# Float32 weights in four column groups of the array for the samples' and adaLN products, and a rebuilt first stretch, in a two-layer hybrid decoder step

## The chip, the cores and the metric

The kernel runs on 1 core of one Trainium2 chip. The metric is the device time in microseconds (us). A NeuronCore has five engines with a queue each: TensorE (PE for its products, PEld for its weight loads), VectorE (DVE), ScalarE (ACT), GpSimd (POOL) and SyncE (SP). SP issues all DMAs here. Every engine works through its own queue in order; semaphores tie them together.

## The reference

One inference step of a two-layer decoder on a prompt of 4096 tokens and on 8 samples of one token each, all in float32, width 1024. What matters here:

```python
shift, scale, gate = split(silu(c) @ ada_w[layer] + ada_b[layer], 3)   # adaLN, 9 rows of c: 8 samples, 1 prompt
h = rmsnorm(x, g_pre) * (1 + scale) + shift
# layer 0: three groups of 4 heads, (window, dilation) = (128,1), (512,4), (2048,16)
q, k, v, z = split(h @ w_in_a, 4);  out = (mixture of the three dilated attentions * silu(z)) @ w_o_a
# layer 1: 16 query heads, 2 shared key/value heads, window 128, sinks
kv = (rmsnorm(x, g_kv) * (1 + kv_scale) + kv_shift) @ w_kv
q, z = split(h @ w_in_b, 2);  out = (attention(q, kv, sinks) * silu(z)) @ w_o_b
x = x + gate * rmsnorm(out, g_post)          # after each layer
```

The prompt and the samples go through the same weights; the samples' keys and values also enter caches that are returned.

## The kernel before

The prompt is cut into 32 tiles of 128 rows. Seven passes follow each other: A0, A1, A2 (layer 0, one head group each: dilation 16, 4, 1), C (the output projection of layer 0), B0, B1 (layer 1, eight query heads each) and D (its output projection). Each pass runs over the 32 tiles. A tile's main work on TensorE is 48 products of 128x128 by 128x512 (36 in C): float16 high and low parts of the activations (`xT`) and weights (`wt`), three products per chunk of 128 input columns, eight chunks, two halves. That makes 32 x (6 x 48 + 36) = 10368 products, written on line 641 (line 634 in the changed file).

The order of the work on every engine is written out by hand. The dictionaries `PA0`, `PA`, `PL`, `PC`, `PB0`, `PB1`, `PD` give each step of a tile a tick; a tile has 48 ticks, in which its 48 products are laid out evenly; step `tq=69` of a tile thus stands in the next tile's ticks. Instructions are issued to the queues in order of ticks. Beside the tiles runs one generator per pass, `side`: all that concerns the 8 samples, the adaLN vectors of later layers, and the splitting of the next pass's weights into float16 parts. It is advanced by one `yield` every `PACE[pi]` ticks, from tile 1 to tile 29; what is left of it when tile 29 ends is issued at once, between two tiles.

The products of the side work have 9 rows of activations (8 samples and the prompt's row). `weights_pass` and `ada_units` load a float32 tile `st` of two chunks of 128x512 weights (512 KB, two buffers), `split_raw` makes from each chunk a high part (ACT, L225) and a low part (POOL, L226) of type fp32r in `wr`, and two products per chunk with a stationary operand of 41 columns (the high parts of the 9 rows in columns 0 to 8, their low parts in 32 to 40) add up in PSUM; `sum_rows` (L215, L218) adds the two row groups of the result. There are 212 such chunks: 64 issued in A0, 48 in A1, 44 in A2, 24 in C (8 of them 256 wide), 16 in B0 and 16 in B1. Where a pass's weights are split, `scan` first reads them all once for their norm (L255).

The first stretch has no tiles to run beside: `begin_loads` fetches the adaLN weights for the first layer's scale and shift (16 x 512 KB); `ada_row` splits them (ACT L465, DVE L466) and makes two rows from them; `begin_scale` reads the weights of A0 for their norm and multiplies them by the shift (`ps_b`, 16 float32 products of full width); `begin_split` makes A0's float16 weights (L299, L300). The first product of tile 0 follows.

At the end of a weights pass the prompt's row of the result goes out to DRAM (`bd`, L408) and comes back spread over 128 partitions (`bias_b`, L414), and DVE takes its maximum (L416): these set the next pass's scales.

## Time and profile before

| | us |
|---|---|
| median of 3 runs | 3180.49 (3174.47 to 3181.64) |
| the profiled execution | 3164.79 |
| its span, first to last instruction | 3162.7 |
| PE / DVE / ACT / POOL busy in the span | 2967.8 / 2248.5 / 1997.1 / 1151.8 |
| mean granted TensorE clock | 0.981 of 2.4 GHz |

A row of the trace that groups instructions reads: line, engine, operation, output<-inputs by the program's names, shapes, count, then busy time and the mean duration of one, then the idle time of that engine just before them and what ended it. A busy time is a union of intervals; products overlap in the pipeline, so the pitch from one start to the next, and not the duration of a record, says what one costs.

### The profile page before, as it was taken

The numbers are of one execution on the slowest core, as the hardware profiler recorded it, in microseconds if no ns is written. First come the engines' busy times: TensorE is split into PE (matmuls) and PEld (weight loads), VectorE is DVE, ScalarE is ACT, GpSimd is POOL, SyncE is SP. The second block draws the span as 40 slices with busy tenths as digits, with TensorE's granted clock in tenths as the row PEclk, the third lists the DMA queues.
The fourth block names the chain that finished last, engine by engine and source line by source line (L and its number), as shares of the span: only waits on it lengthen the run. The fifth ranks groups of instructions, "written<-read, shape, count | busy, mean of one in ns | idle before, by whom it ended". The sixth has DMA issues, their size and how long they took to land.

```text
span 3162.7 us, 54624 instructions
## 1 busy us (share of the span) xinstructions
PE 2967.8 (94%) x18520; PEld 1554.1 (49%) x18520; DVE 2248.5 (71%) x5056; ACT 1997.1 (63%) x4861; POOL 1151.8 (36%) x1284
## 2 busy tenths in 40 slices
PE   6889989999999999988999899999979999999998
PEld 2444444555455444443444455666645555554444
DVE  6666667666677788885676588998866788874443
ACT  6667777566765676766654467766656787763332
POOL 0445533344333566543442123433222343332221
PEclk8999999999999999999999899999999999999999
DMA  8788997677866788769999478665547887888975
GB/s 226 200 214 228 244 242 193 153 167 163 188 147 159 179 197 184 191 148 258 279 256 251 86 168 169 150 136 136 133 110 157 188 178 156 159 193 234 221 203 162
DMA packets 1092677, 585.68 MB, mean 185 GB/s; under 512 B 925014, under 2 KB 1003367, under 8 KB 1089692
## 3 DMA queue, kind: packets, MB, share of 16 engines
q1 hardware_dynamic: 1092396, 582.19, 76.4%
q8 instruction: 145, 2.38, 0.3%
q14 instruction: 136, 1.11, 0.1%
HBM read 243.61 MB, written 159.30 MB: 127 GB/s over the span
## 4 chain that ended last, share of the span: by engine, by line
PE 29%; DVE 9%; ACT 7%; DMA 5%; issue 5%; SPq 2%; POOL 2%; POOLq 0%; ACTq 0%; DVEq 0%
PE ps_pj L641 17%; PE ps_sc L641 6%; DMA PT<-PS 3%; PE ps_sc L99 2%; ACT P L583 2%; PE ps_o L99 2%; DVE PS L592 1%; PE ps_kv L99 1%; SPq L1337 1%; DVE P L576 1%; DVE pn_t L883 1%; DVE x_t L884 1%; ACT PS L591 1%; ACT xs L163 1%; ACT QTb L1008 1%
## 5 line engine op out<-in xcount | busy, mean ns | idle before, releaser
L641 PE MATMUL ps_pj<-wt,xT 128*128 128x512 f16 x9024 | 2226.9, 383 | 43.3 <-ACT ps_pj L624 36.3
L641 PEld LDWEIGHTS <-xT 128*128 128x128 f16 x10368 | 967.8, 98 | 1028.5 <-issue 114.8
L592 DVE SCALAR_TENSOR_TENSOR PS<-P,PS 128x512 f16<-128x512 f32 (+1 forms) x448 | 435.0, 985 | 145.2 <-ACT PS L591 142.7
L544 POOL TENSOR_TENSOR rope<-rope,rope 128x512 f32<-128x512 f32 x160 | 232.9, 1456 | 668.5 <-DVE rope L539 647.5
L226 POOL TENSOR_TENSOR wr<-st,wr 128x512 fp32r<-128x512 f32 (+1 forms) x212 | 310.3, 1464 | 145.8 <-ACT wr L225 145.2
L624 ACT ACTIVATE ps_pj<-bias,scl 128x512 f32<-128x512 f32 x320 | 219.7, 686 | 217.3 <-DVE gate L552 111.7
L583 ACT ACTIVATE P<-P,nm_b 128x256 f32<-128x256 f32 (+1 forms) x512 | 252.7, 494 | 107.1 <-DVE nm_b L576 106.8
L591 ACT ACTIVATE PS<-P 128x512 f16<-128x512 f32 (+1 forms) x448 | 261.4, 598 | 64.4 <-DMA PT<-PS 60.7
L641 PE MATMUL ps_sc<-wt,xT 128*128 128x512 f16 x1344 | 298.4, 379 | 2.5 <-DMA xT<-usdp 1.5
L576 DVE CUSTOM_DVE_ANT_0 P<-ps_sc,masks,nsink 128x256 f32<-128x256 f32 (+1 forms) x512 | 248.9, 527 | 11.8 <-PE ps_sc L99 11.8
L99 PEld LDWEIGHTS <-PT 128*128 128x128 f16 x3384 | 192.4, 99 | 129.6 <-DMA PT<-PS 38.7
L539 DVE SCALAR_TENSOR_TENSOR rope<-ps_pj,scl,tab 128x512 f32<-128x512 f32 x320 | 224.7, 743 | 25.0 <-PE ps_pj L641 24.0
L576 DVE CUSTOM_DVE_ANT_0 P<-ps_sc,masks,scl 128x256 f32<-128x256 f32 (+1 forms) x384 | 155.4, 449 | 65.1 <-PE ps_sc L99 64.8
L609 DVE TENSOR_REDUCE uo<-ps_o 128x256 f32<-128x512 f32 x224 | 153.2, 684 | 53.2 <-PE ps_o L99 51.5
L99 PE MATMUL ps_sc<-KTb,QTb 128*128 128x256 f16 (+1 forms) x1024 | 154.1, 274 | 21.8 <-ACT QTb L1008 15.8
L1051 POOL TENSOR_TENSOR uo<-uo,gate 128x512 f32<-128x512 f32 x64 | 88.4, 1381 | 189.2 <-PE ps_tr L996 83.1
L143 POOL TENSOR_SCALAR rm_t<-ss 128x1 f32<-128x1 f32 (+2 forms) x132 | 34.8, 264 | 329.1 <-ACT xs L163 288.0
L99 PE MATMUL ps_o<-KV,PT 128*128 128x128 f16 x2016 | 129.7, 208 | 21.3 <-DMA PT<-PS 21.2
L736 DVE COPY KT<-ps_tr 64x512 f16<-64x512 f16 x192 | 81.0, 422 | 93.6 <-ACT KT L734 91.3
L769 POOL TENSOR_TENSOR U<-uo,gate 128x256 f32<-128x256 f32 x96 | 93.6, 975 | 140.2 <-DVE uo L609 138.2
L99 PEld LDWEIGHTS <-QTb 128*128 128x128 f16 x1024 | 97.0, 99 | 87.7 <-ACT QTb L1008 27.3
L583 ACT ACTIVATE P<-P,U 128x256 f32<-128x256 f32 (+1 forms) x256 | 118.1, 462 | 34.2 <-DVE U L576 34.1
(257 smaller groups left out, 4055.1 us busy)
## 6 DMA issues: line engine op xcount, KB each, us to landing
out_a_s_dram<-in_cache_a_kv_g_dram SPq DMA_DIRECT2D x144, 256.0 KB
x_t<-in_x_prompt_dram SPq DMA_DIRECT2D x64, 512.0 KB
st<-in_w_in_a_dram SPq DMA_DIRECT2D x96, 256.0 KB
xsd<-xs SPq DMA_DIRECT2D x32, 512.0 KB
st<-in_ada_w_dram SPq DMA_DIRECT2D x32, 512.0 KB
x1d<-x_t SPq DMA_DIRECT2D x32, 512.0 KB
x1s<-xs SPq DMA_DIRECT2D x32, 512.0 KB
st<-in_w_in_b_dram SPq DMA_DIRECT2D x32, 512.0 KB
```

The costliest lines, as they stand in the source:

```text
L99: nc.tensor.matmul(out, lhsT, rhs, start=start, stop=stop)
L226: nc.gpsimd.tensor_tensor(t[:, 1, :n], raw, t[:, 0, :n], op=ALU.subtract)
L539: nc.vector.scalar_tensor_tensor(t[:n, :w].rearrange("p (h e) -> p h e", e=64), s3, scale, tab[:n, o:o + 64].unsqueeze(1).to_broadcast([n, ...
L544: nc.gpsimd.tensor_tensor(a4, a4, b4[:, :, ::-1, :], op=ALU.add)
L576: nc.vector.tensor_tensor_reduce(out=self.P[:, j, :n], in0=self.sc[:, j, :n], in1=self.mask[:, :n], scale=self.nss, scalar=self.init[j], o ...
L583: nc.scalar.activation(self.P[:, j, :n], self.P[:, j, :n], AF.Exp, bias=self.nm[j], scale=-1.0, accum_out=self.l[j])
L591: nc.scalar.activation(S[:, 0], P, AF.Copy, scale=PSC)
L592: nc.vector.scalar_tensor_tensor(S[:, 1], P, PSC, S[:, 0], op0=ALU.mult, op1=ALU.subtract)
L609: nc.vector.tensor_reduce(out=out.rearrange("p (h e) -> p h e", e=64), in_=ops.rearrange("p h (t e) -> p h e t", t=2), axis=AX.X, op=ALU.add)
L624: nc.scalar.activation(t[f"ps{hf}"], bias[pi, hf], AF.Copy, scale=scl[pi][:, IDS:IDS + 1])
L641: nc.tensor.matmul(t[f"ps{hf}"], t[hT][:, p, c, :], ws()[hf][c][q], start=c == 0 and k == 0 and not biased, stop=c == n - 1 and k == 2, sk ...
L769: nc.gpsimd.tensor_tensor(t["U"][:, :256], t["uo"][:, :256], t["sz"][:, :256], op=ALU.mult)
```

## The change

The side work's products take the float32 weights as they are. The stationary operand is 32 columns wide (9 rows and zeros), and four consecutive chunks go to four groups of 32 columns of the array, each into 32 partitions of the same PSUM tile:

```python
def quarter(ps, hS, c, w, nch):
    q = QR * (c % 4)
    nc.tensor.matmul(ps[q:q + QR, :w.shape[-1]], hS[:, c, :], w, start=c < 4, stop=c + 4 >= nch,
                     tile_position=(0, q))

def sum_quarters(ps, rows, width):
    t = s_half()
    nc.scalar.copy(t[:, :width], ps[:, :width])
    yield
    yield
    o = s_half()
    nc.vector.tensor_tensor(t[:64, :width], t[:64, :width], t[64:128, :width], op=ALU.add)
    nc.vector.tensor_tensor(o[:rows, :width], t[:rows, :width], t[QR:QR + rows, :width], op=ALU.add)
    return o
```

```diff
-    stp = ctx.enter_context(tc.tile_pool(name="st", bufs=2))
+    stp = ctx.enter_context(tc.tile_pool(name="st", bufs=4))
-    wrp = ctx.enter_context(tc.tile_pool(name="wr", bufs=2))
...
-PACE = [3, 4, 4, 6, 6, 6, 13]
+PACE = [4, 5, 4, 8, 6, 6, 13]
...
 weights_pass:
-        staged = [jobs[0][-1](), jobs[1][-1]()]
+        staged = [j[-1]() for j in jobs[:4]]
...
-                for k, p in enumerate(parts):
-                    mm(ps[:SROWS, :n], hS[h][:, c + i, :], p, c + i == 0 and k == 0, last and i == 1024 // n - 1 and k == 1)
+            if len(raw) == 4 or last:
+                for k, w in raw:
+                    quarter(ps, hS[h], k, w, max(j[1] + 1024 // n for j in jobs if j[0] == h))
...
 ada_units:
-            for k in range(8):
-                piece(staged, loads, 8 * u + k, got.append)
+            for k in range(0, 8, 4):
+                yield from wait()
+                for c in range(k, k + 4):
+                    quarter(ps, csr, c, staged[4 * u + c // 2][:, c % 2, :], 8)
...
 first stretch:
-        return [(PA0["load"] - 1, begin_loads), (PA0["load"] + 1, begin_rows), (t + 1, begin_scale), (t + 2, begin_rest)] + [
-            (t + 4 + 3 * j, lambda j=j: begin_split(j)) for j in range(16)] + [
-            (t + 12, lambda: [None for _ in first["qkv"]])]
+        return [(PA0["load"] - 1, begin_c), (PA0["load"] + 1, begin_loads), (t + 1, begin_rows), (t + 2, begin_more),
+                (t + 3, begin_scale), (-1, begin_bias), (16, begin_rest)] + [
+            (t + 4 + 3 * j, lambda j=j: begin_split(j)) for j in range(16)]
+    def first_bias(t, hf):
+        t[f"ps{hf}"] = pj_ps.tile([128, 512], F32, name="ps_pj", tag="pj")
+        nc.tensor.matmul(t[f"ps{hf}"], first["spread"], first["t"][hf], start=True, stop=False, skip_group_check=True)
```

In the first stretch `ada_row` takes unsplit weights too (its ACT and DVE splits are gone), the shift times A0's weights is made by quarters (`ps_q`) and spread over the partitions by a product with `spread`, and that product also writes tile 0's bias into PSUM where ACT did it before; 5 of the 16 squares for the norm move from ACT to DVE. The step tables get new ticks in all passes, by up to 10 ticks in `PA0` and one to eight elsewhere; `PACE` is 4, 5, 4, 8, 6, 6 ticks for A0 to B1.

TensorE in the first stretch, before the first main product; `ps_asc`, `ps_apj` are the two adaLN rows, `wa_hl` the split weights, `ps_b` the shift times A0's weights. Before:

```order
L99 MATMUL ps_asc_455<-wa_hl,csr 41x512 x2
L99 MATMUL ps_asc_456<-wa_hl,csr 41x512 x2
...
L99 MATMUL ps_col<-pick,ada_row_370 128x2 x8
L99 MATMUL ps_z<-wa_1_387,ones 128x512 x2
L99 MATMUL ps_b<-st,S_b 128x512 x16
L99 MATMUL ps_scl<-w_acc,ones 128x16
L641 LDWEIGHTS xT
```

And of the change (`wa` are the weights as loaded; `ps_q` stands in the place of `ps_b`):

```order
L210 MATMUL ps_atr_510<-wa_0_427,csr 32x512
L210 MATMUL ps_atr_510<-wa_0_429,csr 32x512
...
L97 MATMUL ps_col<-pick,ada_row_368 128x2 x8
L210 MATMUL ps_q<-st,S_c 32x512 x16
L97 MATMUL ps_scl<-w_acc,ones 128x16
L1506 MATMUL ps_pj<-s_half,spread_s 128x512 x2
L97 MATMUL ps_b<-s_half,spread 128x512 x2
L634 LDWEIGHTS xT
```

The pairs of split products have become single ones, each on another quarter than its neighbour, and two products for the bias stand before the first main product.

SP's queue in the same stretch; `wa` are the adaLN weights, `st` the weights of A0, `xT<-xs` the first transposed activations. Before:

```order
L431 DMA wa_0_403<-in_ada_w_dram 128x1024
L665 DMA x_t<-in_x_prompt_dram 128x1024
L667 DMA tab<-in_rope_dram 128x128
L325 DMA st<-in_w_in_a_dram 128x2x256 x16
L471 DMA adr_G_341<-ada_row_367 41x1024
L471 DMA adr_S_340<-ada_row_370 41x1024
L665 DMA x_t<-in_x_prompt_dram 128x1024
L667 DMA tab<-in_rope_dram 128x128
L179 DMA_TRANSPOSE xT<-xs 128x16x128
```

And of the change:

```order
L424 DMA wa_0_433<-in_ada_w_dram 128x1024
L658 DMA x_t<-in_x_prompt_dram 128x1024
L660 DMA tab<-in_rope_dram 128x128
L174 DMA_TRANSPOSE xT<-xs 128x16x128
L674 DMA xsd_176<-xs 128x2048
L314 DMA st<-in_w_in_a_dram 128x2x256 x16
L464 DMA adr_G_339<-ada_row_365 9x1024 x4
L464 DMA adr_S_338<-ada_row_368 9x1024 x4
```

The first transposing DMA has moved from behind the loads of A0's weights to ahead of them.

DVE at the end of the samples' work in A0, in the change, between tiles 29 and 30; `wt` are float16 weights of A1, `bias_b` the row that came back from DRAM, `V` and `gate` free the second PSUM half of tile 29. These rows stand there:

```order
L289 SCALAR_TENSOR_TENSOR wt<-st,gw,wt 128x512 [waits DMAHW5_49,Activation_49]
L289 SCALAR_TENSOR_TENSOR wt<-st,gw,wt 128x512 [waits Activation_49]
L219 TENSOR_TENSOR s_half<-s_half 64x512 [waits Activation_49]
L220 TENSOR_TENSOR s_half<-s_half 9x512 [waits DVE_49]
L408 TENSOR_REDUCE b_m<-bias_b 128x1 [waits DMAHW4_49]
...
L600 TENSOR_REDUCE uo<-ps_o 128x256 [waits PE_49]
...
L704 SCALAR_TENSOR_TENSOR V<-ps_pj,scl_602,V 128x4x64 [waits Activation_49]
```

Before, the same sum and the same maximum stood a whole tile apart:

```order
L218 TENSOR_TENSOR s_half<-ps_s,s_half 9x512 [waits Activation_49]
L736 COPY KT_957<-ps_tr 64x4x128 [waits Activation_49]
...
L694 TENSOR_TENSOR QK<-rope_5700,QK 128x8x64 [waits Activation_49]
L609 TENSOR_REDUCE uo<-ps_o 128x256 [waits PE_49]
L416 TENSOR_REDUCE b_m<-bias_b 128x1 [waits DMAHW7_49]
```

In A0 the side work of the change is not done when tile 29 ends, and its rest, 6 splits, 8 quarter products and the trip through DRAM, is issued there in one piece.

## Rows read from the trace of the kernel before

**Rows 1.** Busy time of each engine in the seven passes and ahead of them (the stretches begin with a pass's first main product): stretch, its length, PE, PEld, DVE, ACT, POOL busy with counts, granted clock, DMA share, GB/s.

```profile
0.00:68.00 68.00, 43.38 (x142) 18.96 (x143) 40.31 (x88) 46.91 (x89) 3.16 (x12) 0.88 0.86 239
68.00:543.00 475.00, 434.43 (x2553) 213.57 (x2553) 322.95 (x679) 336.51 (x788) 215.28 (x204) 0.97 0.87 220
543.00:971.00 428.00, 421.94 (x2645) 217.23 (x2644) 287.93 (x641) 270.42 (x663) 156.15 (x126) 1.00 0.70 162
971.00:1433.00 462.00, 434.81 (x2689) 222.33 (x2688) 378.44 (x945) 323.72 (x778) 249.12 (x307) 0.99 0.75 177
1433.00:1717.00 284.00, 268.17 (x1253) 120.03 (x1251) 179.09 (x314) 160.55 (x345) 107.99 (x204) 0.98 0.98 267
1717.00:2292.00 575.00, 548.66 (x4145) 337.92 (x4144) 476.04 (x1144) 368.73 (x988) 183.69 (x151) 0.99 0.64 144
2292.00:2814.00 522.00, 479.08 (x3479) 269.59 (x3477) 409.23 (x990) 370.73 (x968) 160.38 (x129) 0.97 0.75 158
2814.00:3163.00 349.00, 337.29 (x1624) 154.50 (x1622) 154.53 (x259) 119.52 (x248) 76.03 (x156) 0.99 0.79 208
```

**Rows 2.** TensorE's instructions by line, tiles and shape: count, then busy us and mean ns of one, then idle before them.

```profile
L641 PE MATMUL ps_pj<-wt,xT 128*128 128x512 f16 x9024 | 2226.9, 383 | 43.3 <-ACT ps_pj L624 36.3 <-DMA xT<-usdp 4.2 <-DVE pn_t L883 2.8
...
L99 PE MATMUL ps_s<-wr,hS 128*41 128x512 f32 x216 | 90.7, 489 | 6.2 <-POOL wr L226 5.3 <-ACT wr L225 0.3
...
L99 PE MATMUL ps_ada<-wr,csr 128*41 128x512 f32 x192 | 80.0, 489 | 5.2 <-POOL wr L226 5.1
...
L99 PE MATMUL ps_b<-st,S_b 128*128 128x512 f32 x32 | 13.9, 592 | 0.0
```

**Rows 3.** The chain of work that ended last, in pass D: start us, us, what.

```profile
2842.84 10.36 PE ps_pj L641 x48
```

**Rows 4.** TensorE in order of time around one chunk of side work in A1: start us, us, engine, line, operation, tiles, shapes, count.

```profile
647.09 1.24 PE L641 MATMUL ps_pj<-wt,xT 128*128 128x512 f16 x5
647.98 0.81 PE L99 MATMUL ps_ada<-wr,csr 128*41 128x512 f32 x2
648.64 1.04 PE L641 MATMUL ps_pj<-wt,xT 128*128 128x512 f16 x4
```

**Rows 5.** All engines in order of time in the first stretch, the same columns; in brackets the idle time before and what ended it.

```profile
3.08 13.21 SPq L431 DMA_DIRECT2D wa<-in_ada_w_dram  x16
...
9.04 11.75 PE L99 MATMUL ps_asc<-wa_hl,csr 128*41 128x512 f32 x32 [0.83 <-ACT wa_hl L465]
...
19.80 14.34 SPq L325 DMA_DIRECT2D st<-in_w_in_a_dram  x16
...
23.87 10.63 PE L99 MATMUL ps_apj<-wa_hl,csr 128*41 128x512 f32 x31 [0.71 <-DVE wa_hl L466]
...
38.27 13.90 PE L99 MATMUL ps_b<-st,S_b 128*128 128x512 f32 x32
...
39.91 13.21 SPq L179 DMA_TRANSPOSE xT<-xs  x1
...
53.54 0.23 DVE L265 TENSOR_TENSOR g<-G0c 128x8 f32<-128x8 f32 x2
...
56.62 3.17 ACT L299 ACTIVATE wt<-st,gw 128x512 f16<-128x512 f32 x5 [7.03 <-DVE gw L1483]
...
68.19 15.83 PE L641 MATMUL ps_pj<-wt,xT 128*128 128x512 f16 x63 [13.63 <-ACT ps_pj L624]
```

**Rows 6.** Groups of instructions of ACT, POOL and DVE by line, columns as in rows 2.

```profile
L226 POOL TENSOR_TENSOR wr<-st,wr 128x512 fp32r<-128x512 f32 (+1 forms) x212 | 310.3, 1464 | 145.8 <-ACT wr L225 145.2
...
L225 ACT CAST wr<-st 128x512 fp32r<-128x512 f32 (+1 forms) x212 | 127.0, 599 | 16.1 <-DMA st<-in_w_in_a_dram 7.1 <-DMA st<-in_ada_w_dram 5.0 <-DMA st<-in_ada_kv_w_dram 2.5
...
L255 ACT ACTIVATE junk<-st 128x512 bf16<-128x512 f32 (+1 forms) x116 | 70.7, 610 | 34.0 <-DMA st<-in_w_in_a_dram 14.9 <-DMA st<-in_w_in_b_dram 10.4 <-DMA st<-in_w_o_b_dram 4.6
...
L466 DVE TENSOR_TENSOR wa_hl<-wa,wa_hl 128x512 fp32r<-128x512 f32 x32 | 20.7, 689 | 1.5 <-ACT wa_hl L465 1.3
```

**Rows 7.** Who waited for whom in the whole span: engine and line that waited, releaser, us in total, times, longest.

```profile
PE ps_pj L641 <- ACT ps_pj L624: 36.3, 13, 13.6
SPq L236 <- POOL wr L226: 79.5, 28, 5.1
POOL s_half L1210 <- DMA s_half<-qsd: 24.5, 7, 6.7
```

**Rows 8.** Two stretches of 20 us in A0 and one behind them, columns as in rows 1.

```profile
200.00:220.00 20.00, 12.94 (x71) 6.28 (x71) 13.60 (x29) 10.13 (x23) 8.03 (x7) 0.83 0.74 177
400.00:420.00 20.00, 12.46 (x56) 5.72 (x55) 7.75 (x18) 15.47 (x42) 3.71 (x4) 0.74 0.91 248
500.00:520.00 20.00, 20.00 (x132) 10.66 (x131) 15.67 (x43) 13.28 (x31) 7.09 (x7) 1.00 0.71 182
```

**Rows 9.** The trip of a bias row through DRAM near the end of A0, in order of time, columns as in rows 4.

```profile
500.71 0.39 SPq L408 DMA_DIRECT2D bd<-s_half  x1
...
502.08 0.37 SPq L414 DMA_DIRECT2D bias_b<-bd  x1
...
506.97 0.67 DVE L416 TENSOR_REDUCE b_m<-bias_b 128x1 f32<-128x512 f32 x1
```

More of the change, by code (lines that the diff above doesn't have):

```diff
@@ L41 @@
-PL = dict(bi0=-6, bi1=19, load=-72, turn=-37, rope=30, sqk=47, vza=50, vzv=60, tq=57, cq=61, tk=61, ck=63, sc0=69,
+PA0 = dict(bi0=-12, bi1=19, load=-113, stat=-81, rstd=-79, high=-72, low=-62, turn=-46, rope=30, sqk=39, vza=58,
+           vzv=62, tq=69, cq=71, tk=63, ck=69, sc0=81, so0=84, ex0=98, pt0=106, tp0=107, sc1=83, so1=87, ex1=103,
+           pt1=104, tp1=119, va0=138, va1=147, sum=149, join=150, store=157)
+PA = dict(bi0=-6, bi1=20, load=-61, turn=-50, rope=28, sqk=50, vza=60, vzv=61, tq=67, cq=72, tk=63, ck=71, sc0=81,
+          so0=85, ex0=92, pt0=99, tp0=107, sc1=82, so1=92, ex1=99, pt1=105, tp1=107, va0=132, va1=135, sum=141,
+          join=144, store=153)
@@ L57 @@
-PACE = [3, 4, 4, 6, 6, 6, 13]
+           denom=115, join=132, store=142)
+PD = dict(load=-98, stat=-77, rstd=-69, high=-60, low=-59, turn=-37, loadx=16, gp=36, sq0=35, sq1=54, rstd2=58,
+          add=67, store=71)
+PACE = [4, 5, 4, 8, 6, 6, 13]
 GAP = [0, 0, 0, 0, 0, 0, 0]
@@ L207, in split_S @@
         yield
[L208 removed]
+        nc.scalar.copy(hS[:, :n, 0:rows], ps[:, :n, :rows])
         yield
@@ L239, in stage_cols @@
         return load
-    def piece(staged, loads, j, out, ahead=2):
-        out(split_raw(staged[j // 2][:, j % 2, :]))
-        if j % 2 and j // 2 + ahead < len(loads):
-            staged.append(loads[j // 2 + ahead]())
     SW, IDS, DS, HD_, DSO, SO, ISO, NSS, FAC = range(9)
@@ L439, in ada_start @@
         nc.vector.memset(ones, 1.0)
-        nc.vector.memset(csr.bitcast(F32), 0.0)
+        nc.vector.memset(csr, 0.0)
+        nc.vector.memset(spread, 0.0)
+        for q in range(4):
+            nc.vector.memset(spread[q * QR:q * QR + 1], 1.0)
         t = xtp.tile([128, D], F32, name="c_t", tag="xt")
@@ L491, in ada_units @@
             loads += [stage_cols([w[:, c0:c0 + 512]], c) for c in range(0, 8, 2)]
-        staged = [ld() for ld in loads[:2]]
+        staged = [ld() for ld in loads[:4]]
         yield from wait()
-        got = []
         for u, (v, i) in enumerate(units):
@@ L501, in ada_units @@
                 dma(g[:n], gvec[i * 512:(i + 1) * 512].unsqueeze(0).to_broadcast([n, 512]))
[L502 to L512 removed]
+            ps = sx_ps.tile([128, 512], F32, name="ps_ada", tag="sx")
+            for k in range(0, 8, 4):
+                yield from wait()
+                for c in range(k, k + 4):
+                    quarter(ps, csr, c, staged[4 * u + c // 2][:, c % 2, :], 8)
+                yield
+                for _ in range(2):
+                    if len(staged) < len(loads):
+                        staged.append(loads[len(staged)]())
+            o = yield from sum_quarters(ps, n, 512)
             yield
@@ L628, in bias_events @@
             ev += [(at["bi0"] - 28, lambda: load_bias(pi, 0)), (at["bi1"] - 46, lambda: load_bias(pi, 1))]
+        if first and not pi:
+            return ev + [(-4, lambda: first_bias(t, 0)), (-3, lambda: first_bias(t, 1))]
         return ev + [(at["bi0"], lambda: put_bias(t, pi, 0)), (at["bi1"], lambda: put_bias(t, pi, 1))]
@@ L1160, in s_start @@
             for i in range(2):
-                a, a2 = (load_s(adr[v][o:o + n, HV[i]]) for o in (0, LO))
+                a, a2 = (load_s(adr[v][q][:, HV[i]]) for q in range(2))
+                yield from wait()
+                nc.gpsimd.tensor_tensor(a, a, a2, op=ALU.add)
+                for q in (2, 3):
+                    a2 = load_s(adr[v][q][:, HV[i]])
+                    yield from wait()
+                    nc.gpsimd.tensor_tensor(a, a, a2, op=ALU.add)
                 b = s_half()
@@ L1483, in begin_scale, with begin_bias @@
         nc.vector.tensor_scalar(first["gw"], G0c, scl[0][:, SW:SW + 1], None, op0=ALU.mult)
-        first["qkv"] = scale_qkv(0, F, bmax)
+        first["t"], first["F"] = t, F
+        first["spread"] = q2.tile([128, 128], F32, name="spread_s", tag="tab", bufs=4)
+        nc.vector.tensor_scalar(first["spread"], spread, scl[0][:, IDS:IDS + 1], None, op0=ALU.mult)
+    def begin_bias():
+        bmax = sm.tile([128, 4], F32, name="b_m", bufs=1)
+        for hf in range(2):
+            pb = tr_ps.tile([128, 512], F32, name="ps_b", tag="tr")
+            mm(pb, spread, first["t"][hf], True, True)
+            bias[0, hf] = bp.tile([128, 512], F32, name=f"bias{hf}", tag="bias")
+            nc.vector.tensor_copy(bias[0, hf], pb)
+            nc.vector.tensor_reduce(out=bmax[:, hf:hf + 1], in_=bias[0, hf], axis=AX.X, op=ALU.max,
+                                    apply_absolute_value=True)
+        for _ in scale_qkv(0, first["F"], bmax):
+            pass
+    def first_bias(t, hf):
+        t[f"ps{hf}"] = pj_ps.tile([128, 512], F32, name="ps_pj", tag="pj")
+        nc.tensor.matmul(t[f"ps{hf}"], first["spread"], first["t"][hf], start=True, stop=False, skip_group_check=True)
     def begin_split(j):
```

159 lines of the change are left out of this document (67 added, 92 removed).

## The prediction

> **What bounds the kernel now.** I read first the busy times of the engines pass by pass [rows 1], because the kernel is seven loops with different limits. TensorE is busy for 95 to 99% of A1, B0, C and D and for 91 to 94% of A0, A2 and B1; the first 68 us are a stretch of their own. DVE comes second, at 82% in A2 and 83% in B0. DMA is near its limit in C (0.98) and high in A0 (0.87). So a microsecond of TensorE work costs or gives about a microsecond, except where A0, A2 and B1 have idle time: 475 - 434 = 41 us, 27 us and 43 us. Then I took the groups of TensorE [rows 2] for what the side work holds there, the chain in D for the undisturbed pitch of a main product [rows 3], TensorE in order of time for what one chunk of side work costs [rows 4], the first stretch [rows 5], and last the groups and waits of the other engines [rows 6, 7].
>
> **What one chunk costs before.** In D 48 main products take 10.36 us, 0.216 us each [rows 3]. In A1 five of them start at 647.09 and would leave the array free at 648.17; the pair of fp32r products stands there, and the next main product starts at 648.64 [rows 4]. The pair costs 0.47 us, although each of its records lasts 0.489 [rows 2]. 204 chunks of full width and 8 of half width make 208 x 0.47 = 98 us of TensorE.
>
> **What one chunk costs after.** A float32 product is not one pass: the 16 products of `ps_b` left 32 records in 13.90 us [rows 2, 5], 0.434 us per record and 0.87 per product. One after the other, four chunks would take 8 x 0.434 = 3.47 us, against 4 x 0.47 = 1.88 before. So the change is dearer on TensorE unless the four column groups work at the same time, and how far they do no row of before shows. Three cases bound it. If all four run together, a group takes two passes, 0.87 us. If none does, 3.47. In between: TensorE starts its products in program order; the two passes of one product need the same 32 columns, so the second follows the first, but the next chunk's first pass has its own columns and can start with it. That gives 1 + 4 passes = 5 x 0.434 = 2.17 us. I take this middle case, since program order is what every stretch of the trace shows.
>
> Going from main products to narrow column groups and back may also need an empty array. A main product's record is 383 ns at a pitch of 216 [rows 2, 3], so emptying it costs at most 0.17 us, twice per group; the fp32r pair shows almost none (0.47 against 2 x 0.216). I take 0.15 per group, between 0 and 0.34. On this the Trainium skill (page "TensorEngine Tiling (Array Packing)", section "Key Properties") says that a change of tiling mode drains TensorE; no run here shows one, and by that rule the whole 0.34 would be paid, 10 us more than I take.
>
> There are 53 groups, two of half width, so 52: 52 x (2.17 + 0.15 - 1.88) = **+23 us**. The ends: all together without emptying, 52 x (0.87 - 1.88) = -53; none together with it, 52 x (3.47 + 0.34 - 1.88) = +100.
>
> **First stretch.** Before, the split of the adaLN weights paces TensorE (`ps_asc` and `ps_apj`, 9.04 to 34.5), the weights of A0 are there by about 38, `ps_b` runs to 52.2, the norm follows, the first split is at 56.62, and tile 0's first product waits until 68.19 for a bias that ACT writes behind 13 splits [rows 5]. After, that bias comes from a product ahead of the splits, and the first product needs one split chunk only. But SP now issues the first transposing DMA ahead of A0's weights, and that one held SP for 13.21 us [rows 5]. I estimate that SP reaches it when the third weight of the second row has landed, near 21 us (16 loads of 512 KB were issued in 13.21 us, each behind the landing of the eighth before it), goes on at 34, and has A0's weights in SBUF near 48; the last group of `ps_q` needs 2.3 us, and squares, norm and scale some 4 (from 48 as from 52.2 to 56.62 before). The first split is then at 52.5 and the first product at 54, 14 us earlier. The transpose may hold SP longer with loads under way, and tile 0 runs at the pace of the splits for a while: I take **-10**, between -18 (nothing held) and +2 (held until 45).
>
> **Waits that go.** TensorE stood 5.3 + 5.1 us for the low parts from POOL [rows 2]; these waits have no successor but the landing of `st`: **-10** (0 to -15, as the clock comes back late after a stop). POOL loses 212 x 1.464 = 310 us and ACT 127 us [rows 6]; both feed TensorE through the rope, the casts and the exponentials. What that gives is a part of the 41 + 27 + 43 us idle in A0, A2 and B1. In A0 the two worst stretches leave TensorE 7 us idle each and drop the granted clock to 0.83 and 0.74, to 1.2 GHz for part of it, where 20 us further on all is full [rows 8]; behind them are side steps that wait on DMAs in an engine's queue (POOL for `qsd` 24.5 us, longest 6.7 [rows 7]; ACT's squares for `st` 14.9 [rows 6]). `PACE` 4 instead of 3 gives each such step a third more time, and four `st` buffers fetch further ahead; SP no longer stands for POOL to free them (79.5 us [rows 7]). I take half of A0's idle time, **-20** (0 to -41), and a fifth of the 70 us in A2 and B1, **-13** (0 to -35).
>
> **What is added.** `sum_quarters` has one DVE addition more per result, 27 x 0.69 us, the duration of such an addition [rows 6], off TensorE's path where DVE has 20% left: 0; without that cover 19 us. The rest of A0's side work in one piece: DVE does 6 splits at 0.69, then stands for the sum and the trip through DRAM, 500.71 to 506.97 = 6.3 us [rows 9], with the evacuation of tile 29's second half queued behind it. TensorE has its quarter groups and the first half of tile 30 (24 x 0.216 = 5.2 us) to do meanwhile and then stands about 6 us, and starts again at the low clock: **+8** (0 to +15). The new ticks in the tables change the order, not the work: 0, between -10 and +10.
>
> **Sum.** +23 - 10 - 10 - 20 - 13 + 8 = -22 us, in the terms of the profiled execution (3164.79). The median of the runs stands 16 us above it, and I carry the difference over: 3180.5 - 22, rounded to 3160 us.
>
> **Rivals.**
>
> All four quarters together. Then 52 x (0.87 + 0.15 - 1.88) = -45 instead of +23, and the first stretch gains its 14: 3160 - 68 - 4 = 3088. For it: nothing in the trace forbids a later instruction with its own columns to start; against it: a product's two passes follow each other in the queue. The Trainium skill ("TensorE: Matmul & The Clock Gate", section "Part 3: Packing small matmuls — row/col tiling") reports three column tiles at 2.38 times the speed, starting some 4 ns apart and in strict program order; that is told of products with one pass, this case has no run of it, and by it two passes in strict order still give my middle case.
>
> No overlap, the other side. The place is every group of four in TensorE's queue. Each then costs 3.47 + 0.15 instead of 1.88: +90 instead of +23, and the rows of the first stretch and `ps_q` take 13.9 us each as `ps_b` did, which eats some 4 us of its gain: 3160 + 67 + 4 = 3231. It decides from a group of about 2.75 us on (52 x 0.42 more than I take eats the 22). For it: the trace has float32 records only one after the other. Against it: only that they there use all columns.
>
> The waits move instead of going. TensorE now waits itself for `st`, where ACT did: 7.1 + 5.0 + 2.5 [rows 6], and loads of 1 MB per group come in bursts in A0, where DMA is high. If none of the 43 us of relief comes and these 15 appear, it is 3180 + 23 - 10 + 8 + 15 = 3216.
>
> The change doesn't do what it says, if the column position has no effect on the records: that is the second rival.
>
> **How the numbers follow.** Middle case 0.42, at 3160 with its own range 3135 to 3190. All together 0.27, no overlap 0.20, waits that move 0.11. A difference within 0.2%, 6 us, is about what a measurement of this kernel cannot tell from none. Faster: the whole 0.27, and 0.33 of the middle case's 0.42, which gives 0.60; within 0.2%: 0.06 of the middle case and 0.04 of the last, 0.10; slower: 0.03 of the middle, 0.20 and 0.07, 0.30. The range 3090 to 3235 leaves half of the first rival (its gain may be larger) and some of the second outside, less than 0.2 together.
>
> **What would show it.** In the profile after, a group of four quarters in A1: from the end of a main product to the start of the next, 2.3 us by my case, near 1.0 or 3.6 by the rivals, with starts of neighbouring quarters 0 or 0.43 us apart. Tiles of A1 with side work longer than those without by 2.3 per group. The first main product near 54 us, and the transposing DMA's hold of SP near 21. A0 shorter by 10 to 30 us, with a stop of some 6 us at tile 30. TensorE's waits for POOL's low parts gone, and none for `st`. I am wrong if A0 keeps its idle time, or if a group takes another time than 2.3.

## The result and the profile after

| us | before | after |
|---|---|---|
| median of the runs | 3177.48 (3172.98 to 3181.64, 4 runs) | 3099.56 (3096.31 to 3104.42, 4 runs) |
| the profiled execution | 3164.79 | 3104.42 |
| its span | 3162.7 | 3102.6 |

The ratio is 0.9756, 95% interval 0.9733 to 0.9779: 78 us faster by the medians, where 22 were forecast. The two profiled executions lie 60.4 apart; the runs of the kernel before scatter from 3166 to 3183 us over all comparisons, and its profiled one lies below them all. The two traces can account for the 60 only.

The changed kernel, stretch by stretch, answers to [rows 1]. The columns are stretch, length, PE, PEld, DVE, ACT, POOL busy with counts, granted clock, DMA share, GB/s.

```profile
0.00:55.50 55.50, 38.57 (x147) 11.89 (x148) 16.32 (x49) 20.25 (x40) 2.70 (x11) 0.91 0.86 292
55.50:524.20 468.70, 421.88 (x2548) 205.06 (x2547) 322.68 (x699) 309.79 (x728) 149.14 (x153) 0.96 0.88 222
524.20:938.10 413.90, 411.62 (x2652) 210.90 (x2651) 281.82 (x649) 249.22 (x619) 95.12 (x78) 1.00 0.75 169
938.10:1393.40 455.30, 426.47 (x2689) 216.38 (x2688) 363.45 (x948) 299.53 (x732) 186.00 (x262) 0.99 0.76 180
1393.40:1668.10 274.70, 261.09 (x1251) 115.80 (x1250) 171.59 (x317) 150.45 (x321) 70.92 (x181) 0.99 0.98 278
1668.10:2241.00 572.90, 544.85 (x4145) 333.93 (x4145) 476.05 (x1146) 358.63 (x971) 156.19 (x134) 0.99 0.67 143
2241.00:2752.50 511.50, 473.46 (x3477) 269.32 (x3476) 391.80 (x988) 358.97 (x950) 148.63 (x113) 0.98 0.77 161
2752.50:3102.00 349.50, 337.49 (x1625) 154.58 (x1623) 155.92 (x262) 120.69 (x250) 76.72 (x156) 1.00 0.79 208
```

Read three sums from it. The first main product starts 12.7 us earlier (68.2 to 55.5). In the seven passes TensorE is busy for 2876.9 us, against 2924.4 before: 47.5 less. Length less busy time, TensorE's idle time, is 169.6 us, against 170.6: as good as unchanged. 12.7 + 47.5 + 1 is the difference. Pass by pass idle time moved a little (A0 41 to 47, B1 43 to 38), but its sum stayed. Each kernel's sum comes from one or two profiles (165.3 us idle in the second one of the change), and busy time is not the work alone: it includes products at half pace after a stop, so that runs with the same products below are busy for 2870 to 2892 us.

TensorE's groups after, as [rows 2]. The side work's 232 + 192 records (16 of them half as wide) take 30.9 + 25.6 us, where 216 + 192 took 90.7 + 80.0, and none of them waits.

```profile
L634 PE MATMUL ps_pj<-wt,xT 128*128 128x512 f16 x9024 | 2202.3, 382 | 32.8 <-ACT ps_pj L615 25.3 <-DMA xT<-usdp 3.7 <-DVE wt L289 3.5
...
L210 PE MATMUL ps_s<-st,hS 128*32 128x512 f32 (+1 forms) x232 | 30.9, 589 | 0.0
L210 PE MATMUL ps_ada<-st,csr 128*32 128x512 f32 x192 | 25.6, 605 | 0.0
```

One group in A1, TensorE in order of time (start us, us, what), as [rows 4]:

```profile
656.27 0.38 PE L634 MATMUL ps_pj<-wt,xT 128*128 128x512 f16 x1
...
656.58 1.07 PE L210 MATMUL ps_ada<-st,csr 128*32 128x512 f32 x8
657.58 0.60 PE L634 MATMUL ps_pj<-wt,xT 128*128 128x512 f16 x2
```

Eight records, two per product, fit in 1.07 us. The main product before them would leave the array free at 656.27 + 0.216 = 656.49; the next starts at 657.58, so four chunks cost 1.09 us where four pairs cost 1.88 [rows 4]. Two passes of 0.43 are 0.87; the other 0.22 is the way in (the first quarter starts 0.31 behind the main product, not 0.216) and out. 52 x (1.09 - 1.88) = -41 us, most of the 47.5.

The first stretch after, SyncE and TensorE apart, as [rows 5]:

```profile
22.16 7.55 SPq L174 DMA_TRANSPOSE xT<-xs  x1
29.76 0.56 SPq L674 DMA_DIRECT2D xsd<-xs  x1
30.37 10.19 SPq L314 DMA_DIRECT2D st<-in_w_in_a_dram  x16
```

```profile
46.26 1.05 PE L210 MATMUL ps_q<-st,S_c 128*32 128x512 f32 x4 [0.39 <-DMA st<-in_w_in_a_dram]
47.53 0.37 PE L97 MATMUL ps_scl<-w_acc,ones 128*128 128x16 f32 x2 [0.22 <-DVE w_acc L255]
50.27 2.65 PE L1506 MATMUL ps_pj<-s_half,spread_s 128*128 128x512 f32 x4 [2.37 <-DVE spread_s L1488]
52.71 2.93 PE L97 MATMUL ps_b<-s_half,spread 128*128 128x512 f32 x4
55.48 9.66 PE L634 MATMUL ps_pj<-wt,xT 128*128 128x512 f16 x44
```

And the end of the side work in A0: TensorE, then DVE, ACT and SyncE, each in order of time.

```profile
491.44 0.81 PE L634 MATMUL ps_pj<-wt,xT 128*128 128x512 f16 x3
503.68 4.00 PE L634 MATMUL ps_pj<-wt,xT 128*128 128x512 f16 x9 [11.43 <-ACT ps_pj L615]
```

```profile
486.72 4.06 DVE L289 SCALAR_TENSOR_TENSOR wt<-st,gw,wt 128x512 f16<-128x512 f32 x6
490.81 0.69 DVE L219 TENSOR_TENSOR s_half<-s_half 64x512 f32<-64x512 f32 x1
491.53 0.68 DVE L220 TENSOR_TENSOR s_half<-s_half 9x512 f32<-9x512 f32 x1
496.72 0.69 DVE L408 TENSOR_REDUCE b_m<-bias_b 128x1 f32<-128x512 f32 x1 [4.50 <-DMA bias_b<-bd]
...
499.53 0.68 DVE L600 TENSOR_REDUCE uo<-ps_o 128x256 f32<-128x512 f32 x1
...
502.04 0.48 DVE L704 SCALAR_TENSOR_TENSOR V<-ps_pj,scl,V 128x256 f16<-128x256 f32 x1 [0.63 <-ACT kvo L699]
```

```profile
501.16 0.47 ACT L697 ACTIVATE gate<-ps_pj,scl 128x256 f32<-128x256 f32 x1 [8.72 <-POOL U L762]
502.94 0.69 ACT L615 ACTIVATE ps_pj<-bias,scl 128x512 f32<-128x512 f32 x1 [0.94 <-DVE gate L543]
```

```profile
492.24 0.24 SPq L400 DMA_DIRECT2D bd<-s_half  x1
493.38 0.34 SPq L406 DMA_DIRECT2D bias_b<-bd  x1
```

DVE makes six splits, sums the quarters, stands 4.5 us for the trip through DRAM and does the scales. Only then comes `uo`, for which ACT has been standing by way of POOL, and at 502.04 tile 29's V. When V and the gate have emptied their PSUM half, ACT writes the next bias into it and TensorE goes on. It has stood for 11.43 us, and its next nine products take 4.00 us, twice their usual pitch (granted clock 0.50, that is 1.2 GHz, from 503.6 to 507.5). Tile 30 takes 26.3 us from first product to first product, where it took 12.0 before. This stop is the longest of the second of these two waits, which answer to [rows 7]:

```profile
PE ps_o L97 <- DMA PT<-PS: 36.4, 25, 5.3
PE ps_pj L634 <- ACT ps_pj L615: 25.3, 10, 11.4
```

The first of them, for the transposing DMA of `PT`, was 25.8 us before. In A0 alone it grew from 2.0 to 14.8 us, while the 8.1 us that TensorE stood for POOL's low parts there are gone: a part of the idle time only changed its cause.

### The profile page after: what moved, and what is told of

Same layout as the page of the kernel before. It is cut to its first block, busy times and chain, and to the rows that moved or that the text cites. A ratio compares the mean times of both kernels' runs of the same rounds, so it can differ in the third digit from the quotient of the medians.

```text
span 3102.6 us, 53900 instructions
## 1 busy us (share of the span) xinstructions
PE 2915.4 (94%) x18524; PEld 1517.9 (49%) x18524; DVE 2179.6 (70%) x5053; ACT 1867.5 (60%) x4606; POOL 885.4 (29%) x1085
## 3 DMA queue, kind: packets, MB, share of 16 engines
q14 instruction: 132, 1.07, 0.1%
## 4 chain that ended last, share of the span: by engine, by line
PE 39%; DVE 6%; DMA 6%; ACT 5%; issue 4%; SPq 2%; POOL 1%; ACTq 0%; POOLq 0%; DVEq 0%
PE ps_pj L634 23%; PE ps_sc L634 8%; DMA PT<-PS 3%; PE ps_sc L97 3%; PE ps_o L97 2%; ACT P L574 2%; DMA xT<-usdp 2%; DVE PS L583 1%; SPq L1335 1%; PE ps_kv L97 1%; DVE P L567 1%; ACT PS L582 1%; ACT QTb L1001 1%; PE ps_s L210 1%; DVE rope L530 1%
## 5 line engine op out<-in xcount | busy, mean ns | idle before, releaser
L634 PE MATMUL ps_pj<-wt,xT 128*128 128x512 f16 x9024 | 2202.3, 382 | 32.8 <-ACT ps_pj L615 25.3
L583 DVE SCALAR_TENSOR_TENSOR PS<-P,PS 128x512 f16<-128x512 f32 (+1 forms) x448 | 403.6, 921 | 104.3 <-ACT PS L582 101.9
L535 POOL TENSOR_TENSOR rope<-rope,rope 128x512 f32<-128x512 f32 x160 | 252.2, 1576 | 767.1 <-DVE rope L530 739.9
L567 DVE CUSTOM_DVE_ANT_0 P<-ps_sc,masks,nsink 128x256 f32<-128x256 f32 (+1 forms) x512 | 249.6, 528 | 13.0 <-PE ps_sc L97 12.7
L762 POOL TENSOR_TENSOR U<-uo,gate 128x256 f32<-128x256 f32 x96 | 102.1, 1064 | 260.7 <-DVE uo L600 242.7
L142 POOL TENSOR_SCALAR rm_t<-ss 128x1 f32<-128x1 f32 (+1 forms) x132 | 32.6, 247 | 341.2 <-ACT xs L158 284.1
L97 PE MATMUL ps_sc<-KT,QT 128*128 128x256 f16 (+1 forms) x768 | 111.3, 265 | 16.6 <-DVE KT L729 14.6
```

What stands on the lines that cost most here:

```text
L97: nc.tensor.matmul(out, lhsT, rhs, start=start, stop=stop)
L535: nc.gpsimd.tensor_tensor(a4, a4, b4[:, :, ::-1, :], op=ALU.add)
L567: nc.vector.tensor_tensor_reduce(out=self.P[:, j, :n], in0=self.sc[:, j, :n], in1=self.mask[:, :n], scale=self.nss, scalar=self.init[j], o ...
L583: nc.vector.scalar_tensor_tensor(S[:, 1], P, PSC, S[:, 0], op0=ALU.mult, op1=ALU.subtract)
L634: nc.tensor.matmul(t[f"ps{hf}"], t[hT][:, p, c, :], ws()[hf][c][q], start=c == 0 and k == 0 and not biased, stop=c == n - 1 and k == 2, sk ...
L762: nc.gpsimd.tensor_tensor(t["U"][:, :256], t["uo"][:, :256], t["sz"][:, :256], op=ALU.mult)
```

## The experiments

All are read against the kernel before, timed on the same chip. The last column is the ratio less that of the changed kernel (0.9768 where it ran beside them), times 3172 us. By the two intervals together, up to about 7 us of it (8 for e1 to e4, whose intervals are wider) is not told from nothing.

| run | median us | ratio, 95% interval | us against the change |
|---|---|---|---|
| after_again | 3097.46 | 0.9768 (0.9753 to 0.9783) | |
| e1_one_quarter | 3203.59 | 1.0088 (1.0064 to 1.0112) | +102 |
| e2_pace3 | 3116.41 | 0.9812 (0.9792 to 0.9831) | +14 |
| e3_weights_first | 3093.62 | 0.9742 (0.9721 to 0.9763) | -8 |
| e4_dummy_splits | 3133.39 | 0.9867 (0.9847 to 0.9887) | +31 |
| e5_old_tables | 3128.50 | 0.9866 (0.9851 to 0.9880) | +31 |
| e6_pace36 | 3096.57 | 0.9767 (0.9751 to 0.9783) | 0 |
| e7_eights | 3097.48 | 0.9770 (0.9752 to 0.9788) | +1 |
| e8_copies_later | 3093.90 | 0.9760 (0.9746 to 0.9773) | -3 |
| e9_old_tables_dummy | 3167.69 | 0.9986 (0.9975 to 0.9997) | +69 |
| e10_first_and_copies | 3088.45 | 0.9737 (0.9722 to 0.9751) | -10 |
| e11_rest_in_tile_30 | 3097.63 | 0.9768 (0.9752 to 0.9784) | 0 |
| e12_before_new_tables | 3163.63 | 0.9968 (0.9956 to 0.9980) | (-10 against before) |
| e13_dummy_scalar | 3111.66 | 0.9811 (0.9798 to 0.9824) | +14 |
| e14_dummy_gpsimd | 3120.90 | 0.9838 (0.9824 to 0.9851) | +22 |
| e15_late_rest | 3079.47 | 0.9716 (0.9702 to 0.9730) | -16 |
| e16_old_ticks_new_pace | 3129.32 | 0.9872 (0.9858 to 0.9885) | +33 |

> The changed kernel itself, unchanged, beside the three below on the same chip, as the point from which they are read: 3100 us within 8 by every theory.

### Do the four quarters work at the same time?

```diff
-                    quarter(ps, csr, c, staged[4 * u + c // 2][:, c % 2, :], 8)
+                    one_quarter(ps, csr, c, staged[4 * u + c // 2][:, c % 2, :], 8)
```

`one_quarter` writes `ps[:QR]` at `tile_position=(0, 0)` for every chunk, in `weights_pass` too.

> All 52 groups of four chunks go to the same 32 columns of the array, one after the other, with the same weights, loads, order and tables; only the first stretch keeps its quarters, and the two additions over the quarters go. Theory 1, that the gain comes from four quarters working at the same time: a group takes 8 passes of 0.434 us and some 0.2 us around them, 3.67 us where the change takes 1.09, so 52 x 2.6 = +134 us, about 3234 us. Theory 2, that the gain is the relief of ScalarE and GpSimd and the longer groups fill time in which TensorE is idle anyway: at most +60, about 3160 or less.

TensorE in A1 with one quarter:

```profile
676.72 0.38 PE L635 MATMUL ps_pj<-wt,xT 128*128 128x512 f16 x1
677.03 3.62 PE L214 MATMUL ps_ada<-st,csr 128*32 128x512 f32 x8
680.59 0.60 PE L635 MATMUL ps_pj<-wt,xT 128*128 128x512 f16 x2
```

The same eight records now take 3.62 us, the group 680.59 - 676.94 = 3.65, as expected. Theory 1 holds: the column groups are the gain, and without them the kernel would be slower than before. +102 instead of +134, because idle time (length less busy, from the first main product on) fell from 165.3 to 140.8 us: part of the longer groups filled waits, as theory 2 had it, but the smaller part.

```diff
-            for k in range(0, 8, 4):
+            for c in ((0, 4, 1, 5, 2, 6, 3, 7) if v in ("G1", "GP1") else range(8)):
```

> The adaLN products of A0 and A1 are issued in groups of eight in the order of chunks 0 to 7, those of A2 in the order 0, 4, 1, 5, 2, 6, 3, 7, so that neighbours use the same 32 columns. Theory 1, four quarters advance together and a group pays about 0.22 us once for getting in and out: a group of eight costs 4 x 0.434 + 0.22 = 1.96 us in A1 (2 x 1.09 = 2.18 before), the whole saves 3 to 6 us. In A2, if TensorE starts its products in program order and a product waits until its columns are free, neighbours on the same columns follow each other and only unlike neighbours meet: 5 x 0.868 + 0.22 = 4.6 us; if it takes them out of order by columns, 1.96 there too.

TensorE in A2, with neighbours on the same columns:

```profile
1055.18 1.03 PE L635 MATMUL ps_pj<-wt,xT 128*128 128x512 f16 x4
1056.13 1.95 PE L210 MATMUL ps_ada<-st,csr 128*32 128x512 f32 x16
1058.01 0.39 PE L635 MATMUL ps_pj<-wt,xT 128*128 128x512 f16 x1
```

16 records in 1.95 us, where A1, in the order 0 to 7, has 1.92. The single records start in four volleys 0.43 us apart, four in each, 7 ns from one to the next in A1 and 13 ns in A2. A product whose columns are taken does not hold up the one behind it that has others: each column group works off its own passes. This is what the forecast had excluded. A group of eight saves 2 x 1.09 - 1.95 = 0.2 us, twelve of them under 3 us, which does not show in the time.

### What ScalarE and GpSimd lost

```diff
                 raw.append((c + i, v[:, i]))
+                split_raw(v[:, i], n)
```

`split_raw` casts the chunk to a scratch tile (ScalarE) and writes a subtraction to another (GpSimd); nobody reads them. e13 keeps the first line of it alone, e14 the second.

> Every one of the 212 chunks of the side work gets its cast on ScalarE (128x512) and a subtraction on GpSimd (128x448) again, whose results nobody reads; TensorE's work is the change's. This gives ScalarE some 127 us and GpSimd some 270 us back. Theory 1: these engines' relief is worth little, since nothing on TensorE waits for the results: +0 to +8 us. Theory 2, the prediction's: the relief of the two engines is what shortens the idle time in A0, A2 and B1, and to give the work back costs 25 to 35 us.

> The changed kernel with the 212 dummy casts on ScalarE alone, without the subtractions on GpSimd. Theory 1, the relief is ScalarE's, which evacuates the PSUM banks that TensorE waits for: +25 to +34 us, as much as both together. Theory 2, it is GpSimd's, whose subtractions hold up rope and the release of st: 0 to +10.

> The changed kernel with the 212 dummy subtractions on GpSimd alone, without the casts on ScalarE. Theory 1 (ScalarE's relief): 0 to +10 us. Theory 2 (GpSimd's relief): +25 to +34 us.

Theory 2 of the first holds: +31. GpSimd's share is the larger one (+22 and +14, so neither of the two theories that gave it all to one engine holds). The idle time of TensorE from the first main product on is 194.0 us with both, 185.6 with GpSimd's part and 171.9 with ScalarE's, against 165.3 in the changed kernel's second profile. One way in which a subtraction on GpSimd can reach TensorE shows in DVE's groups, of the change and then of the run with GpSimd's part:

```profile
L583 DVE SCALAR_TENSOR_TENSOR PS<-P,PS 128x512 f16<-128x512 f32 (+1 forms) x448 | 403.6, 921 | 104.3 <-ACT PS L582 101.9
...
L289 DVE SCALAR_TENSOR_TENSOR wt<-st,gw,wt 128x512 f16<-128x512 f32 (+1 forms) x88 | 64.5, 749 | 8.1 <-ACT wt L288 8.0
```

```profile
L592 DVE SCALAR_TENSOR_TENSOR PS<-P,PS 128x512 f16<-128x512 f32 (+1 forms) x448 | 416.7, 950 | 103.4 <-ACT PS L591 101.2
...
L295 DVE SCALAR_TENSOR_TENSOR wt<-st,gw,wt 128x512 f16<-128x512 f32 (+1 forms) x88 | 76.5, 885 | 7.6 <-ACT wt L294 7.5
```

The same split takes DVE 885 ns instead of 749 (975 in the kernel before, 751 with ScalarE's casts alone). In all, DVE is busy for 2211 us instead of 2164 from the first main product on, with not one instruction of its own more. The Trainium skill ("SBUF — State Buffer", section "Who interferes with whom") says that a DVE instruction with two inputs in SBUF contends with a GpSimd instruction that reads SBUF. Both groups have two such inputs, and the trace agrees: of the 88 splits the 31 that overlap a subtraction last 1169 ns in the mean and the other 57 731, while the rope products, with one input in PSUM, last 747 and 744. How much of the 22 us comes this way is not shown: the subtractions also fill GpSimd's own queue for 240 us, ahead of its other steps, and no run separates the two. Of ScalarE's 14 us the runs show the size alone.

### The step tables

```diff
-PACE = [4, 5, 4, 8, 6, 6, 13]
+PACE = [3, 4, 4, 6, 6, 6, 13]
```

With it, in e5 and e9, go all of `PA0` to `PD` of the kernel before; e16 has those tables and the change's `PACE`; e9 adds the dummy load of e4; e12 is the kernel before with the change's tables and its own `PACE`.

> The changed kernel with the step tables and PACE of the kernel before; quarters, four st buffers and the order of the first stretch stay. Theory 1: the tables only order the work, and the gain is that of the quarters: 3100 within 10 us. Theory 2: the slack that the relief of ScalarE and GpSimd makes has to be taken up by the ticks, which were set for the old load: without the new ones 15 to 30 us of the gain go, 3115 to 3130.

> The changed kernel with the step tables PA0 to PD of the kernel before, but its own PACE (4, 5, 4, 8, 6, 6). The side work has fewer steps than before (378 instead of 450 in A0, 244 instead of 346 in A1), so that with the old PACE it stood closer together. Theory 1: that density is most of the 31 us that old tables and old PACE cost together; with the new PACE only B1's 12 us are left, 3105 to 3113. Theory 2: it is the ticks: 3118 to 3130.

> The step tables and PACE of the kernel before together with the dummy casts on ScalarE and subtractions on GpSimd for each of the 212 chunks. The tables alone cost +31 us, the dummy work alone +34. Theory 1, two separate gains: both together cost 60 to 65 us, 3158 to 3165. Theory 2, one gain: the relief is only collected where the ticks are set for it, and with the old ticks the dummy work fits as the split work did before: 3125 to 3140.

> The kernel before with the step tables PA0 to PD of the change, its own PACE, its split products and its first stretch. Theory 1, the tables are a gain of their own, independent of the quarters: 10 to 25 us under the kernel before, in B1 above all (its last tile 15 instead of 20 us). Theory 2, they only fit the new load: 0 to +20 us.

The tables are worth 31 us (theory 2), and in sum it is the ticks, not the pace (e16, theory 2). By pass, old against new tables: A0 475.3 against 462.6, A1 421.4 against 411.9, B1 522.1 against 509.7, the others within 5. The sum hides two things. In A1 the new pace with the old ticks gives 414.2, most of the gain there, while in A0 it costs 10 us (485.1). And A0's tiles 0 to 28 take 409.3 us instead of 439.4, of which the last three, with the stop, give 17 back. Old ticks and the dummy load together cost 69, 7 more than one by one, so the two are separate gains (theory 1 of e9, a little above its range). In the kernel before, the new ticks give 10 us, the lower edge of theory 1: they bring B1 from 521.7 to 510.7 us but lengthen A0, A1, A2 and C by 3 to 7 us each. So about a third of the 31 us comes with the old load too, and the rest is a fit to the new one.

e9 is the most telling of all: new products and new first stretch with about the old load and the old ticks, and it is 0.14% faster than before. Its row from the first main product to the end, columns as above:

```profile
56.00:3158.00 3102.00, 2887.23 (x18379) 1505.04 (x18377) 2209.23 (x5005) 1951.04 (x4778) 1102.48 (x1286) 0.98 0.77 184
```

TensorE is busy for 37 us less than before (2924.4), and the first product comes 12 us earlier, but its idle time is 3102.00 - 2887.23 = 214.8 us, 45 more. What the column groups gave was eaten by waits. With the load gone (e5) the idle time is 190.4, with the new ticks as well 165 to 170.

### A0: the stop, the DMA engines, the first stretch

```diff
-PACE = [4, 5, 4, 8, 6, 6, 13]
+PACE = [3, 5, 4, 8, 6, 6, 13]
...
+        if pi == 0 and it == NB - 2 and s % 2 == 1:
+            pump(sides[pi])
...
-            if it == NB - 3:
+            if it == NB - (2 if pi == 0 else 3):
```

The first two lines are e2 (in e6 the 3 is 3.6), the others e11.

> A0's side work is advanced every 3 ticks again instead of 4, so that it is done before tile 29 ends; nothing else changes. Theory 1: the rest of the side work that stands in one piece after tile 29 costs the 11.4 us stop at tile 30 and its low clock, together 14 us; without it the time falls by 10 to 14 us, to about 3088. Theory 2: the earlier side steps find their data later and stop the engines elsewhere in A0, as they did before the change; the stop is only moved, 3100 within 5 us.

> A0's side work (378 steps, 348 of which fit in tiles 1 to 29 at one per 4 ticks) is advanced once in 3.6 ticks, so that it just fits and nothing is issued in one piece behind tile 29; nothing else changes. Theory 1: the stop of 11.4 us at tile 30 goes and the earlier tiles keep most of the looser pace: -8 to -14 us against the changed kernel on the same chip. Theory 2: as with 3 ticks, the stop comes back as smaller ones in the earlier tiles: no gain, -2 to +10.

> The changed kernel, but what is left of A0's side work after tile 29 (30 of 378 steps) is spread over tile 30, one step every 2 ticks, instead of being issued in one piece; tiles 1 to 29 keep their pace. Theory 1: the stop of 11.4 us at tile 30 goes and nothing earlier gets denser, tile 30 takes 14 to 17 us instead of 25 to 26: -8 to -11 us against the changed kernel, near 3088. Theory 2, as with the pace of 3.6: the stop moves, to tile 31 or to the start of A1, whose scales wait for the same trip through DRAM: within 4 us.

Three times the stop only moves, as theory 2 has it, and with 3 ticks the cost is above both theories. With 3 and 3.6 ticks there is no stop at tile 30, but ones of 2 to 5 us all along A0 (473.3 and 465.9 us against 462.6). With 3 ticks A0's idle time is no longer than in the change (44.3 and 45.6 us); TensorE is busy for 12 us more with the same products, at a mean granted clock of 0.95 instead of 0.97. So a stop also costs the slow products behind it, which idle time does not show. With the rest in tile 30 the stop stands at tile 31, 8.3 us, with DVE again waiting for the bias row (6.05 us).

```diff
-            if copies and n >= 2 and order[pi][0] != "c":
+            for _ in range((0, 2, 1, 0, 1, 1, 1)[pi]):
...
+    def begin_raw():
+        first["raw"] = [j[-1](wp, "w") for j in feeds[0].jobs]
...
-                (t + 1, begin_rows),
+                (t - 1, begin_raw), (t + 1, begin_rows),
```

The copies behind a tile, by pass, are e8; the loads in a step of their own, ahead of the transpose at `t`, are e3; e10 has both.

> The 30 copies of cache blocks (256 KB each, from input to output in DRAM) that SyncE issues behind the tiles of A0 are left to A1, which issues two behind each tile; nothing else changes. In A0 the DMA engines move 104 MB and are busy 0.88 of the time, 1.02 in its second half; the copies are 7.5% of that. Theory 1: TensorE's 45 us of idle time in A0, which stayed between 44 and 50 us at every pace and with either set of tables, are DMA time; A0 gets 10 to 25 us shorter, the total falls by 8 to 20 us against the changed kernel. Theory 2: the idle time is the order of steps in the engines' queues: within 4 us of the changed kernel (3097 to 3100).

> In the first stretch the 16 loads of A0's weights are issued behind the adaLN loads, ahead of the first transposing DMA, which held SyncE from 22.16 to 29.71 us. Theory 1: the weights land some 6 us earlier (last product of ps_q near 39 instead of 44 us), the first main product is near 50 instead of 55.5, and the time falls by about 4 us. Theory 2: the transposing DMA, now issued near 33 us under full load, is late itself (it held SyncE for 13.21 us before the change), and tile 0 waits for it: first product at 53 or later, no change within 3 us.

> A0's weights loaded ahead of the first transposing DMA, and no copies in A0, together. Theory 1: two separate gains, 4 to 6 us and 8 to 20, together 12 to 25 us under the changed kernel, 3073 to 3087. Theory 2: what A0 loses at its start it waits for later, because it is bound by DMA from end to end: no more than e8 alone.

Without copies A0 gets 5.5 us shorter (457.1), its idle time goes from 45.6 to 39.2, and TensorE's wait there for the transposing DMA of `PT` is 8.4 us (16.2 in the change's second profile). But A1 gets 3 us longer, and of the total only 3 us are left, which is not told from nothing (theory 2). DMA is a part of A0's idle time; as the copies are only 7.5% of its traffic, the run does not show how large a part. With the weights first, the transposing DMA starts at 37.68 and holds SyncE 4.97 us, and the first product is at 53.4, not at 50. It does not follow the transpose, as theory 2 had it, but the bias products with `spread`, which run from 46.98 to 53.40, at a mean granted clock of 0.54. The -8 is not told from the change with certainty. Both together are 10 us faster than the change, their intervals just apart: the sum of the two alone, less than theory 1 had and more than theory 2.

```diff
+        k = s + (it - NB + 2) * TICKS
+        if pi == 0 and k >= 0 and (k % 3 < 2 if k < 21 else k % 4 == 0):
+            pump(sides[pi])
```

This stands on top of e10, and in A0 nothing is issued in one piece any more.

> A0's weights ahead of the first transposing DMA and no copies in A0 (as in e10_first_and_copies), and the last 30 steps of A0's side work spread over tiles 30 and 31: the six splits and eight products fast, then one step every 4 ticks, so that four steps of waiting stand between the load of the bias row and its maximum. Theory 1: with some 16 ticks (4 us) for the trip, DVE stands 2 us at most, tiles 30 and 31 together take 27 to 29 us instead of 37: 8 to 10 us under e10, 3078 to 3081. Theory 2: the stop only moves, as it did to tile 31: within 4 us of 3088.

TensorE and then DVE where the stop was:

```profile
504.89 0.81 PE L634 MATMUL ps_pj<-wt,xT 128*128 128x512 f16 x3 [2.22 <-ACT ps_pj L615]
```

```profile
499.76 0.69 DVE L408 TENSOR_REDUCE b_m<-bias_b 128x1 f32<-128x512 f32 x1 [2.65 <-DMA bias_b<-bd]
```

The stop of 11.4 us is now one of 1.9 and one of 2.2; tiles 30 and 31 take 30.6 us together (27 to 29 were expected), where e10 has 37.2. e11, which spreads the same steps without this distance, kept a stop of 8.3. So the trip through DRAM in front of DVE's evacuation was its cause. At 3079.47 us this version is faster than both kernels; its gain over e10 alone (0.9716 against 0.9737, 7 us) is a little under the expected 8 to 10 and not beyond the intervals.

## Why the prediction was right and wrong

The direction was right, the size wrong: 22 us forecast, 60 in the profiled executions, 78 by the medians. Against the sum of the trace:

| us | forecast | measured |
|---|---|---|
| first product | -10 | -12.7 |
| TensorE's work in the passes | +23 | -47.5 |
| its idle time (waits that go -10, A0 -20, A2 and B1 -13, stop +8) | -35 | -1 |
| median less profiled execution, change of it | 0 | -17 |

**One chunk after: the step that failed.** A group of four was put at 2.17 + 0.15 us and takes 1.09, so a term of +23 stands where the groups gave -41. That "the next chunk's first pass has its own columns and can start with it" was right, but "TensorE starts its products in program order" was carried one step too far: that the second pass of a product blocks the products behind it. The records of the change (four starts 7 ns apart) and e7 show that it does not, and e1 what the far case costs (3.65 us). The rule cited for it, strict program order, was weighed as if it held between columns; no row of this case bore it out, and that it is told of products with one pass stands nowhere in the Trainium skill. The entry and exit, 0.22, lie within the bounds 0 to 0.34. The rival with all four together had the mechanism and nearly the group (0.87 + 0.15). That its time, 3088, came within 12 us was luck: it too counted 35 us of idle time that did not go, and the shift of the median, which nobody had forecast, made up for 17 of them.

**First stretch.** The first product came at 55.5, not 54, but two errors met there. SyncE reached the transpose at 22.16 (21 expected) and was held for 7.55 us, not 13.21, so that the last group of `ps_q` ended near 47, 3 us ahead of the forecast. But the first product then waited for the bias products with `spread`, which have it start without ACT: they fill TensorE from 50.27 to 55.48, in part at half pace, and the sum had no term for them.

**Waits for POOL.** Gone, and nothing waits for `st` instead. The rival with waits that move had the wrong place, but its other condition, that none of the 43 us comes, is what the sum of idle time shows.

**Relief: the second step that failed.** The 33 us were about right as the worth of the relief (e4: 31), in A2 (452.8 against 467.7 us) as much as in A0 (462.6 against 475.4), but wrong as a term: they do not come off the idle time that [rows 1] show. A0 kept its idle time, which the prediction had named as a sign of being wrong: POOL's 8.1 us and 7.5 of `QT`'s wait went, the stop and 13 us more for the transposing DMA of `PT` came. A reading that fits, though no run shows it by itself: when TensorE's share of a tile gets shorter by what it saves, the other engines' steps come due earlier; e9 has 45 us more idle time than before. The relief and the new ticks paid that back. The terms were added as if each were independent of the others.

**Tables.** Taken at 0 between -10 and +10, with the argument that they change "the order, not the work". e5 and e16 show 31 to 33 us. Where TensorE is busy for 94% of the span and DVE for 70%, the order decides how much of the rest is waiting.

**The stop.** Right in place and cause; 11.43 us, not 6, and 14 in all (26.3 against 12.0), the products behind it at half pace. The tail behind the trip (scales, `uo`, V, gate) had been left out.

**Median.** To carry the 16 us between profile and median of the kernel before over to the other kernel cost 17: the changed kernel's median lies 5 us below its profile and the kernel before's 13 above.

What stays open: which of the new ticks do it in A0, how much of GpSimd's part goes through DVE, why the evacuation and the transposing DMAs come late in A0 outside the stop (some 12 and 15 us of TensorE's idle time there), and what the four `st` buffers are worth, which no run took back alone.

## What to carry to other kernels

A saving on the engine that is nearly full is only worth what the others can follow: look at its idle time after, at the pace of its products behind each stop, and at which steps come due earlier. Work that is taken off an engine with time to spare can still be worth its removal, through what it shared with another (GpSimd's subtractions slowed DVE). And a trip through DRAM whose result a shared engine waits for belongs far ahead of the next thing that this engine has to empty.
